# Half-head mixers, resident output weights and one query pass in a decoder-layer kernel

## Chip, cores and metric

The kernel runs on one core of a Trainium2 chip. The metric is device time of one launch, in microseconds (us). All tensors are float32; products that must be accurate are made from a high and a low part (three matmuls, `mm3`).

## What is computed

One layer of a decoder for 1,024 prompt tokens and 64 sample tokens (8 sequences of 8), cut to what matters here:

```python
proj = rmsnorm(h) @ w_in                      # retention and RWKV-7 columns
o_ret = head_norm(retention(q, k, v)) * silu(g)          # 8 heads of 64
o_rw  = (head_norm(rwkv7(r, w, k, kk, a, v)) + bonus) * g2   # 8 heads of 64
h = h + concat(o_ret, o_rw) @ w_out
xn = rmsnorm(h)                               # PEER:
s  = (xn @ wq) . keys                         # 8 heads, two halves of 128 keys
e  = 16 best of the pairs, per head           # 128 experts of 16,384 per token
h  = h + sum_e gate_e * gelu(xn . pu[e]) * pv[e]
h  = h + sigmoid(h' @ w_gate) * (p @ w_ple);  final rmsnorm
```

The RWKV-7 step is done in chunks of 128 tokens: per head a triangular system is solved level by level (blocks double in size), and a state is carried to the next chunk.

## The kernel before

The 1,088 tokens are nine tiles: 0 to 7 are the prompt (128 tokens each), 8 is the sample (64). Three stages follow one another.

**Projections (0 to about 600 us).** `group_a` makes the projections of tiles 0 and 1, 2 and 3, then 4 to 8 (lists `A0`, `A1`, `A2`). `a_ret` writes retention columns to DRAM (`rd`), `a_rw` the RWKV columns, transposed, to `fd`. Tile 0's mixer (`first_mix`) is interleaved with the second group. `c_rows` then does tile 0's output projection, residual and norm and writes the normed rows `xd`; `early` starts on that tile beside the third group.

**Mixers (`group_b`, about 600 to 1868 us).** Tiles are mixed in the order `BORDER` = 1, 8, 2, 3, ..., 7. `mixers` is `ret_mix` (load `qv`, retention, half of the output row) and then `rw_mix` (load `ft`; decay, keys and masks; the solve; state; norm; the other half). Two tiles are in flight: the one whose solve runs (`cur`) and the one that is prepared up to the solve (`nxt`). All eight heads of a tile are worked together, in tiles of 128x1024 or 128x512. A level of the solve (line 837 and on) does four heads after the other four: a transpose of Z into `Tt`, the products `pG` and `pZG`, and two VectorE steps (`G`, `Z`). The mixer's output row goes to DRAM (`od`) in two halves, and `c_rows` loads it back (`cot`) and multiplies it with `w_out`, of which it loads sixteen pieces of 256 KB (`cw`, line 609) per tile.

**The early tiles.** Tiles 0, 1 and 8 (`E0`) don't go through the dense expert pass at the end: for each of their tokens' 128 experts a row of `pu` and later one of `pv` is gathered from HBM by GpSimd (`gather`, line 1126) and used by VectorE (line 1140 for `pu`, 1154 for `pv`). Before that, `early_query` streams the query weights (sixteen times 512 KB, `ewq`, and a key block `ekT`) and makes the scores, and `topk` picks the experts. In `group_b` one step of `early` is taken per step of the mixers, at most `EB` = 150. Gathered rows have four places: two in `V`, one in `W`, one in `xy`. Tile 0's query has two weight buffers (`V`); those of tiles 1 and 8 run one after the other with one buffer (`Wq`), beside tile 0's gathers, each once its tile's rows are there (`rowed`).

**The rest (1868 us to the end).** Queries, top-k, gates and hidden products of tiles 2 to 7, the dense expert passes `ph` and `py` of tiles 4 to 7, and beside them the rest of the gathers, for tiles 2 and 3 too; then the per-layer embedding.

The order of the instructions on each engine is fixed when the program is built, by a scheduler that takes them in program order and by priorities; `early` has a later priority. On the chip each engine runs its list in order. SyncE (SP) issues most loads, in its own fixed order.

Of the kernel before, what the change touches and what calls it, by code (L numbers as in the profile page):

```python
# [17 lines left out]
D = 1024  # L18
# [167 lines left out]
IB = 2  # L186
PGT = "a"
SPL = "gv"
IE = 2
IA = 2  # L190
G2 = [4, 5, 6, 7]
RSTART = 2
RRATE = 1
# [17 lines left out]
class K:  # L211
# [28 lines left out]
    def setup(self):  # L240
# [11 lines left out]
        self.od = {t: self.dp.tile([128, D], F32, name=f"od{t}") for t in range(9)}  # L252
        self.yd = {t: self.dp.tile([128, D], F32, name=f"yd{t}") for t in range(9)}
        self.fd = self.dp.tile([128, 14, T], F32, name="fd")
# [3 lines left out]
    def setup_mix(self, es):  # L258
# [18 lines left out]
        self.Sb = [[cp.tile([128, 4, 128], F32, name=f"S{a}{b}") for b in range(2)] for a in range(3)]  # L277
# [60 lines left out]
    def group_a(self, pools, tiles, tags, then=None):  # L338
# [16 lines left out]
        yield from self.a_ret(wp, tiles, x, prepare(), tags)  # L355
        yield "rw"
        yield from self.a_rw(wp, tiles, x, tags)

    def a_ret(self, wp, tiles, x, ready, tags):
        nc, I = self.nc, self.I  # L360
        off, _ = spans(tiles)
        if True:
            for cb in range(8):
# [8 lines left out]
                if cb == 0:  # L372
                    next(ready, None)
# [30 lines left out]
    def head_norm(self, wp, p, n, eps, mk):  # L404
        nc = self.nc
        pv = p[:n].rearrange("p (h d) -> p h d", h=8)
        s = wp.tile([128, 8], F32, name="hns")
        nc.vector.tensor_reduce(s[:n], pv, axis=AX.X, op=OP.add)
        nc.vector.tensor_scalar(s[:n], s[:n], 1.0 / 64, None, op0=OP.mult)
        xc = mk("hnx").rearrange("p (h d) -> p h d", h=8)  # L410
        nc.vector.tensor_tensor(xc[:n], pv, s[:n, :, None].to_broadcast([n, 8, 64]), op=OP.subtract)
        sq = mk("hnq").rearrange("p (h d) -> p h d", h=8)
        nc.scalar.activation(sq[:n], xc[:n], AF.Square)
        ss = wp.tile([128, 8], F32, name="hnss")
        nc.vector.tensor_reduce(ss[:n], sq[:n], axis=AX.X, op=OP.add)
        r = self.rsq(wp, ss, n, 1.0 / 64, eps, 8, "hnr")
        nc.vector.tensor_tensor(xc[:n], xc[:n], r[:n, :, None].to_broadcast([n, 8, 64]), op=OP.mult)
# [18 lines left out]
    def ret_mix(self, wp, t):  # L436
# [3 lines left out]
        rt = dict(qv="Q", qkT="Z", inT="N", hnx="Tt0", hnq="Tt1") if t == 0 else dict(hnx="qkT", hnq="inT")  # L440
# [3 lines left out]
        q, k, v, gt = (qv[:n, j * 512:j * 512 + 512] for j in range(4))  # L444
        qT = mk("qkT", [128, 8, n])
        for kk in range(2):
            p = self.ps("tr").rearrange("p (a b) -> p a b", a=4)
            for j in range(4):
                nc.tensor.transpose(p[:, j, :n], qv[:n, (kk * 4 + j) * 128:(kk * 4 + j) * 128 + 128], self.c("ident")[:n, :n])
            nc.scalar.activation(qT[:, 4 * kk:4 * kk + 4, :n], p[:, :, :n], AF.Copy)  # L450
            yield
# [1091 lines left out]
```

## Time and profile before

| | us |
|---|---|
| median of three runs | 3939.46 (3925.63 to 3940.68) |
| profiled execution, its own time | 3941.76 |
| its span | 3940.0 |
| TensorE busy | 3367.7 (85%) |
| VectorE busy | 2961.7 (75%) |
| GpSimd busy | 2339.6 (59%) |
| ScalarE busy | 1225.5 (31%) |
| mean granted TensorE clock, share of full | 0.87 |
| data moved | 1107.20 MB, mean 281 GB/s |

Shares are of the whole span; the stages differ. A stretch is read from the table of windows (busy time of each engine, granted clock), what was late in it from the waits (who waited, for whom) and from the chain, which follows the work that ended last back to what released it.

### The profile page before, as it was taken

Reading aid. Unit: us, or ns where it says so; the run is one execution under the profiler, and the core shown is the slowest. Engines: PE = TensorE matmul, PEld = TensorE weight load, DVE = VectorE, ACT = ScalarE, POOL = GpSimd, SP = SyncE. Lnnn points to the kernel's source line nnn. Section 1 sums busy time; section 2 is a strip of 40 time slices with the busy share of each in tenths; the row PEclk is TensorE's granted clock in tenths of the full one; section 3 lists DMA queues with packets and bytes.
Section 4 is the critical chain, followed back from the end, with each engine's and each line's share of the span. In section 5 each row is a group of like instructions: output and inputs, shape, how many; then the busy total and the mean of one; then the engine's idle time right before and its main releaser. Section 6 shows DMA issues by size and latency. Waiting matters only on the chain.

```text
span 3940.0 us, 52682 instructions
## 1 busy us (share of the span) xinstructions
PE 3367.7 (85%) x17749; PEld 2768.7 (70%) x17749; DVE 2961.7 (75%) x5764; ACT 1225.5 (31%) x2247; POOL 2339.6 (59%) x2051
## 2 busy tenths in 40 slices
PE   8798985777869776885899899999699988999978
PEld 7687984645747664763788678888588866677757
DVE  4454488977697689886659999987777777777774
ACT  4232221011111111111232266777422333333322
POOL 5353175544454536554567757886488777777740
PEclk9799995666977567676999999999899999999989
DMA  7267568898868878789998748899899999999962
GB/s 256 72 194 234 168 209 266 277 302 267 295 229 285 299 269 283 265 278 332 331 350 295 245 171 302 306 347 344 324 343 341 334 362 357 358 362 349 339 230 70
DMA packets 473864, 1107.20 MB, mean 281 GB/s; under 512 B 74555, under 2 KB 191545, under 8 KB 467642
## 3 DMA queue, kind: packets, MB, share of 16 engines
q0 software_dynamic: 165888, 604.05, 43.0%
q1 hardware_dynamic: 245694, 393.26, 30.5%
q10 hardware_dynamic: 62012, 106.52, 7.2%
q8 instruction: 141, 2.31, 0.2%
q14 instruction: 129, 1.06, 0.1%
HBM read 997.17 MB, written 106.43 MB: 280 GB/s over the span
## 4 chain that ended last, share of the span: by engine, by line
PE 45%; DVE 22%; DMA 16%; issue 7%; POOL 6%; ACT 2%; SPq 0%; ACTq 0%; POOLq 0%; DVEq 0%
PE py L1294 14%; DVE grow L1140 4%; DVE gacc L1154 3%; PE ph L325 3%; PE ph L326 3%; PE ph L327 3%; POOL grow L1126 3%; DMA ewq<-in_wq 2%; PE epq L1194 2%; DMA grow<-in_pv,eid 2%; DMA grow<-in_pu,eid 2%; POOL vl L300 2%; DMA ft<-fd 1%; DVE oh L1240 1%; PE ewo L610 1%
## 5 line engine op out<-in xcount | busy, mean ns | idle before, releaser
L1126 POOL DMA_INDIRECT grow<-in_pv,eid x576 | 569.8, 989 | 507.3 <-DVE gacc L1154 309.4
L1126 POOL DMA_INDIRECT grow<-in_pu,eid x576 | 568.7, 987 | 435.2 <-DVE grow L1140 287.9
L1154 DVE SCALAR_TENSOR_TENSOR gacc<-grow,ac,gacc 128x1024 f32<-128x1024 f32 x571 | 731.8, 1282 | 89.5 <-DMA grow<-in_pv,eid 84.3
L1140 DVE SCALAR_TENSOR_TENSOR grow<-grow,gacc 128x1024 f32<-128x1024 f32 x576 | 691.1, 1213 | 125.0 <-DMA grow<-in_pu,eid 118.3
L1294 PE MATMUL py<-ah,vh 128*128 128x512 f32 x1024 | 408.1, 399 | 40.3 <-ACT ah L296 27.1
L1294 PE MATMUL py<-ah,vl 128*128 128x512 f32 x1024 | 407.1, 403 | 34.1 <-POOL vl L300 34.0
L325 PE MATMUL ph<-cx,uh 128*128 128x512 f32 x1024 | 406.4, 397 | 7.2 <-ACT geh L1262 7.2
L326 PE MATMUL ph<-cx,uh 128*128 128x512 f32 x1024 | 406.4, 397 | 0.0
L327 PE MATMUL ph<-cx,ul 128*128 128x512 f32 x1024 | 405.5, 396 | 1.0 <-POOL ul L300 1.0
L1294 PE MATMUL py<-al,vh 128*128 128x512 f32 x1024 | 405.3, 396 | 0.0
L300 POOL TENSOR_TENSOR vl<-vraw,vh 128x640 fp32r<-128x640 f32 (+2 forms) x224 | 325.4, 1457 | 53.1 <-ACT vh L296 49.3
L300 POOL TENSOR_TENSOR ul<-uraw,uh 128x1024 fp32r<-128x1024 f32 x128 | 308.6, 2412 | 64.5 <-ACT uh L296 62.3
L296 ACT ACTIVATE vh<-vraw 128x640 fp32r<-128x640 f32 (+2 forms) x224 | 154.9, 692 | 393.8 <-PE py L1294 238.3
L1294 PEld LDWEIGHTS py<-ah,vl 128*128 128x128 f32 x1024 | 194.1, 190 | 98.4 <-POOL vl L300 56.1
L1294 PEld LDWEIGHTS py<-ah,vh 128*128 128x128 f32 x1024 | 194.6, 190 | 96.5 <-ACT vh L296 28.7
L1298 DVE TENSOR_TENSOR yT<-yT,py 128x512 f32<-128x512 f32 x216 | 147.4, 684 | 151.5 <-PE py L1294 151.1
L325 PEld LDWEIGHTS ph<-cx,uh 128*128 128x128 f32 x1024 | 194.7, 190 | 48.4 <-ACT geh L1262 8.8
L1294 PEld LDWEIGHTS py<-al,vh 128*128 128x128 f32 x1024 | 194.0, 189 | 43.7
L327 PEld LDWEIGHTS ph<-cx,ul 128*128 128x128 f32 x1024 | 194.9, 190 | 41.6 <-POOL ul L300 1.9
L326 PEld LDWEIGHTS ph<-cx,uh 128*128 128x128 f32 x1024 | 195.0, 190 | 39.1
L296 ACT ACTIVATE uh<-uraw 128x1024 fp32r<-128x1024 f32 x128 | 135.2, 1056 | 246.1 <-PE ph L326 128.5
L300 POOL TENSOR_TENSOR wl<-wraw,wh 128x1024 fp32r<-128x1024 f32 x45 | 110.5, 2455 | 138.8 <-ACT wh L296 138.7
(400 smaller groups left out, 7833.3 us busy)
## 6 DMA issues: line engine op xcount, KB each, us to landing
uraw<-in_puT SPq DMA_DIRECT2D x128, 512.0 KB, 4.8
vraw<-in_pvd SPq DMA_DIRECT2D x152, 320.0 KB, 6.1
cw<-in_w_out SPq DMA_DIRECT2D x128, 256.0 KB, 5.1
wd<-wst ACTq DMA_DIRECT2D x32, 1024.0 KB, 13.1
wt<-wd SPq DMA_DIRECT2D x64, 512.0 KB, 8.0
wraw<-in_w_ret SPq DMA_DIRECT2D x48, 512.0 KB, 4.7
ewq<-in_wq SPq DMA_DIRECT2D x48, 512.0 KB, 6.7
gd<-geh ACTq DMA_DIRECT2D x96, 256.0 KB, 5.0
```

The lines of the kernel that those rows point to most:

```text
L296: nc.scalar.activation(hi, src, AF.Copy)
L300: nc.gpsimd.tensor_tensor(lo, src, hi.bitcast(F32), op=OP.subtract)
L325: mm(out, lh(k), rh(k), start=first and k == 0, stop=False)
L326: mm(out, lh(k), rl(k), start=False, stop=False)
L327: mm(out, ll(k), rh(k), start=False, stop=last and k == nk - 1)
L610: nc.tensor.matmul(p[:n], oT[k // 4][:, k % 4, :n], w, start=k == 0, stop=k == 7)
L1126: nc.gpsimd.indirect_dma_start(out=g, out_offset=None, in_=src, in_offset=bass.IndirectOffsetOnAxis(ap=self.eid[t][:, j:j + 1], axis=0))
L1140: nc.vector.scalar_tensor_tensor(g[:, c], g[:, c], 1.0, x[:, c], op0=OP.mult, op1=OP.mult, accum_out=hv[:, i, j:j + 1])
L1154: nc.vector.scalar_tensor_tensor(y[:, c], g[:, c], ac[:, j:j + 1], y[:, c], op0=OP.mult, op1=OP.add)
L1194: nc.tensor.matmul(p[:, :n], w[:, k], xT[:, k, :n], start=k == 0, stop=k == 7)
L1294: nc.tensor.matmul(p, lh[:, b, :], rh, start=b == 0 and j == 0, stop=b == nb - 1 and j == 2)
L1298: nc.vector.tensor_tensor(yT[:, d, :], yT[:, d, :], p, op=OP.add)
```

## The change

- A mixer's unit is now half of a tile's heads: `ret_mix` and `rw_mix` take (tile, half `g`), their tiles are half as wide, in two buffers (`BB`), and a level of the solve is one group of four heads. Two units are in flight, as two tiles were. One set of pools (`mix_pools`) serves tile 0 and `group_b`.
- The output row stays on chip (`ot`, 128x1024, two buffers): the stores to `od` and the loads `cot` are gone.
- `w_out` is loaded once in `group_b` (`wo`, eight pieces of 512 KB); only tile 0's `c_rows` still loads `cw`. All tiles but 7 end their `c_rows` in `group_b`.
- `fd` is laid out by tile, so that a tile's columns are contiguous: a load `lo` of two column blocks for both halves, `ft` of six for each half. The order of the blocks in `a_rw` (`FT`) and of the column groups in `a_ret` changes with it.
- Gathered rows have seven places in `group_b`: three of the pool `rows` (`R2`) beside the four. After the queries two more (`W2`), and for the last tile `xT`.
- Tiles 1 and 8 share one query pass: three weight buffers, each weight block used for both tiles. It begins when the rows of both are there; `group_b` takes no step of `early` until then.
- `RR` = 2 steps of `c_rows` per mixer step, from the start; `IB` 3 for 2.

In numbers of instructions: VectorE 4,542 to 4,861, GpSimd 2,056 to 2,184, ScalarE 2,609 to 2,656, TensorE 14,633 to 14,651, SP 1,098 to 972.

The core of the diff:

```diff
-IB = 2
-PGT = "a"
+IB = 3
+FT = (12, 13, 4, 5, 0, 1, 8, 9, 6, 7, 2, 3, 10, 11)
 SPL = "gv"
+BB = 2
+R2 = 3
+RR = 2
...
-RSTART = 2
-RRATE = 1
...
-        self.fd = self.dp.tile([128, 14, T], F32, name="fd")
+        self.fd = self.dp.tile([9, 128, 14, 128], F32, name="fd")
...
-    def ret_mix(self, wp, t):
+    def ret_mix(self, wp, t, g):
...
-        qv = mk("qv", [128, RET])
-        nc.sync.dma_start(qv[:n], self.rd[t][:n])
+        qv = mk("qv", [128, 4, 256])
+        nc.sync.dma_start(qv[:n], self.rd[t][:n].rearrange("p (j c) -> p j c", j=4)[:, :, g * 256:g * 256 + 256])
...
-        nc.scalar.dma_start(self.od[t][:n, :512], xf)
+        if g == 0:
+            self.ot[t] = (self.ep0.tile([128, D], F32, name="ot", tag="Wq", bufs=1) if t == 7 else
+                          self.mp.tile([128, D], F32, name="ot", bufs=2))
+        nc.vector.tensor_tensor(self.ot[t][:n, 256 * g:256 * g + 256], xf, gt, op=OP.mult)
...
-        for k in range(1 if t == 7 else 2):
-            nc.sync.dma_start(ot[k][:n], self.od[t][:n, cs[k]])
...
                 for k in range(8):
-                    w = half("cw")
-                    nc.sync.dma_start(w, I['w_out'][k, :, cs[c]])
+                    if self.wo:
+                        w = self.wo[k][:, cs[c]]
+                    else:
+                        w = half("cw")
+                        nc.sync.dma_start(w, I['w_out'][k, :, cs[c]])
                     nc.tensor.matmul(p[:n], oT[k // 4][:, k % 4, :n], w, start=k == 0, stop=k == 7)
...
+    def mix(self, tiles):
+
+        nxt = None
+        units = [(t, g) for t in tiles for g in range(2)]
+        for i, u in enumerate(units + [None]):
+            cur, nxt = nxt, self.mixers(*u) if u else None
+            live = nxt is not None
+            while live or cur is not None:
+                if cur is not None:
+                    if next(cur, "end") == "end":
+                        cur = None
+                        if units[i - 1][1]:
+                            self.mixed.append(units[i - 1][0])
+                if live:
+                    live = next(nxt, "end") != "chain"
+                yield
 
     def group_b(self, tiles, early):
...
+            for k in range(8):
+                wo.append(wp.tile([128, D], F32, name=f"wo{k}"))
+                self.nc.sync.dma_start(wo[k], self.I['w_out'][k])
+            self.wo = wo
+            for _ in self.mix(tiles):
+                for _ in range(RR):
+                    if next(rows, "end") == "end" and self.mixed and self.mixed[0] != 7:
+                        rows = self.c_rows(self.co, self.mixed.pop(0))
+                for _ in range(ERATE if self.rowed.issuperset(E0) else 0):
+                    if steps < EB:
+                        steps += 1
+                        next(early, None)
...
-        ft = wp.tile([128, 14, n], F32, name="ft")
-        nc.sync.dma_start(ft, self.fd[:, :, o:o + n])
...
+            lo = wp.tile([128, 2, n], F32, name="lo")
+            nc.sync.dma_start(lo, self.fd[t, :, 0:2, :n])
...
+        ft = wp.tile([128, 6, n], F32, name="ft", bufs=2)
+        nc.sync.dma_start(ft, self.fd[t, :, 2 + 6 * g:8 + 6 * g, :n])
...
-            for s in range(2):
-                p = self.ps("trz", hb[s]).rearrange("p (a b) -> p a b", a=4)
-                for j in range(4):
-                    nc.tensor.transpose(p[:n, j, :n], Z[:n, 4 * s + j, :n], self.c("ident", n)[:, :n])
...
+            p = self.ps("trz", "b").rearrange("p (a b) -> p a b", a=4)
+            for j in range(4):
+                nc.tensor.transpose(p[:n, j, :n], Z[:n, j], self.c("ident", n)[:, :n])
...
-    def early_query(self, wp, t, wtag, wbufs, stags):
+    def early_query(self, wp, tiles, ws, xts):
...
-            for k in range(8):
-                nc.tensor.matmul(p[:, :n], w[:, k], xT[:, k, :n], start=k == 0, stop=k == 7)
...
+            for t in tiles:
+                for k in range(8):
+                    nc.tensor.matmul(p[:, off[t]:off[t] + SIZE[t]], w[:, k], xT[t][:, k, :SIZE[t]], start=k == 0, stop=k == 7)
...
+        while not self.rowed.issuperset(E0):
+            next(g, None)
+            yield
+        w2 = (self.r2, "W2", 2)
+        for _ in self.early_query(wp, E0[1:], [(wp, "Wq", 1), w2, w2], [(wp, "xT", 1), (self.r2, "R", R2)]):
+            next(g, None)
+            yield
         for t in E0[1:]:
-            while t not in self.rowed:
+            for _ in self.early_topk(wp, t, [w2, w2]):
                 next(g, None)
                 yield
-            for _ in self.early_query(wp, t, "Wq", 1, ("Wq", "xT")):
-                next(g, None)
-                yield
+        self.rows += [w2, w2]
         yield from g
...
+            r2 = self.r2 = sb("rows", ew, side="right")
+            self.layout(r2, [("R", [128, D], F32, R2), ("W2", [128, D], F32, 2)])
+            self.rows += [(r2, "R", R2)] * R2
             late = self.group_b(BORDER, early)
```

VectorE, the mixers of tiles 1 and 8. Before, in tile 1's solve (`G`, `Z`), while tile 8 is prepared; `grow` on line 1140 is the use of a gathered `pu` row of tile 0:

```order
L851 TENSOR_TENSOR Z<-Z,pZG 128x128x2
L1140 SCALAR_TENSOR_TENSOR grow,hv<-grow,gacc 128x1024
L461 TENSOR_TENSOR inT<-pin,cstb 64x256 x2
L1140 SCALAR_TENSOR_TENSOR grow,hv<-grow,gacc 128x1024
L851 TENSOR_TENSOR Z<-Z,pZG 128x128x2
L1140 SCALAR_TENSOR_TENSOR grow,hv<-grow,gacc 128x1024
L844 TENSOR_TENSOR G_6726<-pG,cstb 128x256
L1140 SCALAR_TENSOR_TENSOR grow,hv<-grow,gacc 128x1024
L431 SCALAR_TENSOR_TENSOR qm<-qkT,cstb 128x512 x2
L1140 SCALAR_TENSOR_TENSOR grow,hv<-grow,gacc 128x1024
L844 TENSOR_TENSOR G_6768<-pG,cstb 128x256
```

The change, tile 8's second half in its solve, tile 2's first half prepared:

```order
L417 TENSOR_REDUCE hnss<-hnq 64x4
L876 TENSOR_TENSOR G<-pG,cstb 64x128
L463 TENSOR_TENSOR inT<-pin,cstb 128x256 x2
L419 TENSOR_TENSOR hnx<-hnx,hnr 64x256
L882 TENSOR_TENSOR Z<-Z,pZG 64x64x2
L410 TENSOR_REDUCE hns<-po 128x4
L511 TENSOR_TENSOR S_192<-pst,S_193 64x2x64 x2
L411 TENSOR_SCALAR hns<-hns 128x4
L512 TENSOR_TENSOR S_192<-S_192,cstb 64x2x64 x2
L876 TENSOR_TENSOR G<-pG,cstb 64x128
L413 TENSOR_TENSOR hnx<-po,hns 128x256
L1008 TENSOR_TENSOR ot<-hnx,pgt 64x256
```

The gathered rows of tile 0 are no longer between these steps: 74 of its 128 `pu` rows are used by the end of tile 1's first half, and the 75th comes after both halves of tile 8.

TensorE, the query pass (`epq`: with `ewq` the query, with `ekT` the scores). Before, tile 1's, beside tile 8's state products (`pss`, `psT`):

```order
L1194 MATMUL epq<-exT,ewq 128x128 x8
L1197 MATMUL epq<-ekT,eqT 128x128
L943 MATMUL pss<-uexp,nbk 64x512
L943 MATMUL pss<-uexp,ktk 64x512
L950 MATMUL psT<-csta,sw_7809 64x64 x8
L1194 MATMUL epq<-exT,ewq 128x128 x8
L761 MATMUL pbon<-cstb,sq 128x8 x4
L761 MATMUL pbon<-cstb,rk_7843 128x8 x4
L1197 MATMUL epq<-ekT,eqT 128x128
```

The change, tiles 1 and 8 together, beside tile 2's solve and preparation:

```order
L1234 MATMUL epq<-exT,ewq 128x128 x8
L1234 MATMUL epq<-exT,ewq 128x64 x5
L1241 MATMUL epq<-ekT,eqT 64x128
L1234 MATMUL epq<-exT,ewq 128x64 x3
L880 MATMUL pZG<-G,Tt 128x64 x4
L756 MATMUL pcs<-cstb,sg 128x129 x2
L1241 MATMUL epq<-ekT,eqT 128x128
L869 MATMUL trz<-csta,Z 128x128 x4
L874 MATMUL pG<-Z,N 128x64 x4
L1234 MATMUL epq<-exT,ewq 128x128 x8
L1234 MATMUL epq<-exT,ewq 128x64 x2
L1241 MATMUL epq<-ekT,eqT 64x128
```

Each weight block is now used for 128 and for 64 columns, one behind the other; before, tile 8's sixteen blocks came in a second pass.

SP, the beginning of `group_b`. The change:

```order
L535 DMA wraw<-in_w_rw 128x1024 x3
L1228 DMA ekT<-in_keysT 128x128 x2
L535 DMA wraw<-in_w_rw 128x1024 x11
L701 DMA wo_6582<-in_w_out 128x1024
L701 DMA wo_6584<-in_w_out 128x1024
L701 DMA wo_6586<-in_w_out 128x1024
L701 DMA wo_6588<-in_w_out 128x1024
L701 DMA wo_6590<-in_w_out 128x1024
L701 DMA wo_6592<-in_w_out 128x1024
L701 DMA wo_6594<-in_w_out 128x1024
L701 DMA wo_6596<-in_w_out 128x1024
L446 DMA qv<-rd_112 128x4x256
L732 DMA lo<-fd 128x256
L742 DMA ft<-fd 128x768 x2
L446 DMA qv<-rd_112 128x4x256
```

The eight loads of `wo` stand behind the projections' last weights (`wraw`) and ahead of tile 1's loads.

## Rows read from the trace of the kernel before

**Rows 1.** The page: busy time (share) xinstructions; chain that ended last

```profile
PE 3367.7 (85%) x17749; PEld 2768.7 (70%) x17749; DVE 2961.7 (75%) x5764; ACT 1225.5 (31%) x2247; POOL 2339.6 (59%) x2051
...
PE 45%; DVE 22%; DMA 16%; issue 7%; POOL 6%; ACT 2%; SPq 0%; ACTq 0%; POOLq 0%; DVEq 0%
```

**Rows 2.** Windows: stretch, length, busy us by engine, PEclk, DMA share, GB/s

```profile
600.00:1868.00 1268.00, 951.99 (x4988) 736.82 (x4989) 1006.97 (x1874) 176.31 (x379) 646.47 (x638) 0.68 0.83 280
600.00:930.00 330.00, 237.05 (x1199) 168.48 (x1200) 269.57 (x476) 39.66 (x87) 174.67 (x173) 0.62 0.86 277
930.00:1060.00 130.00, 101.68 (x706) 85.31 (x704) 88.65 (x109) 19.64 (x47) 55.08 (x54) 0.81 0.90 285
1290.00:1420.00 130.00, 109.54 (x485) 98.12 (x486) 79.92 (x148) 16.64 (x43) 56.29 (x59) 0.51 0.83 288
1509.00:1729.00 220.00, 187.05 (x1026) 147.90 (x1025) 190.43 (x274) 39.81 (x77) 123.92 (x119) 0.76 0.83 284
100.00:200.00 100.00, 77.38 (x529) 69.43 (x527) 47.41 (x89) 26.23 (x47) 31.48 (x28) 0.78 0.23 73
1868.00:3940.00 2072.00, 1900.23 (x8826) 1541.02 (x8824) 1641.69 (x3196) 873.30 (x1560) 1418.50 (x1154) 0.97 0.86 308
```

**Rows 3.** The chain of waits from 600 to 1870 us, by line

```profile
by line: issue 8.4%; DMA ewq<-in_wq 6.9%; DVE grow L1140 6.6%; DMA grow<-in_pv,eid 5.7%; PE epq L1194 5.3%; DVE gacc L1154 4.9%; DMA grow<-in_pu,eid 4.5%; DMA ft<-fd 4.2%; POOL grow L1126 3.6%; PE ewo L610 3.0%; DMA cw<-in_w_out 2.8%; PE pZ
```

**Rows 4.** The same chain, one piece: start us, length us, what

```profile
602.48 12.95 DMA ft<-fd
```

**Rows 5.** Windows of L1126 (gather issues) alone: GpSimd busy us (xissues)

```profile
600.00:1868.00 1268.00, 480.60 (x480) 0.68 0.83 280
```

**Rows 6.** VectorE groups, 600-1870 us: busy us, mean ns | idle before

```profile
L1154 DVE SCALAR_TENSOR_TENSOR gacc<-grow,ac,gacc 128x1024 f32<-128x1024 f32 x246 | 315.1, 1281 | 57.7 <-DMA grow<-in_pv,eid 55.9
L1140 DVE SCALAR_TENSOR_TENSOR grow<-grow,gacc 128x1024 f32<-128x1024 f32 x233 | 280.4, 1212 | 61.0 <-DMA grow<-in_pu,eid 59.4
L844 DVE TENSOR_TENSOR G<-pG,cstb 128x256 f32<-128x256 f32 x70 | 29.2, 417 | 29.4 <-PE pG L842 29.1
L851 DVE TENSOR_TENSOR Z<-Z,pZG 128x256 f32<-128x256 f32 x70 | 28.6, 413 | 11.2 <-PE pZG L849 10.6
...
L798 DVE TENSOR_TENSOR Kq<-pab,cstb 128x512 f32<-128x512 f32 x28 | 18.9, 682 | 8.2 <-PE pab L793 8.2
```

**Rows 7.** TensorE waits, same stretch: us, times, longest us

```profile
PE epq L1194 <- DMA ewq<-in_wq: 22.6, 15, 6.9
...
PE ewo L610 <- DMA cw<-in_w_out: 10.6, 10, 3.6
...
PE etr L594 <- DMA cot<-od: 7.2, 3, 3.1
```

**Rows 8.** TensorE groups, same stretch

```profile
L610 PE MATMUL ewo<-cw,coT 128*128 128x512 f32 x192 | 107.3, 667 | 8.0 <-DMA cw<-in_w_out 6.3 <-DVE S L506 0.7 <-DVE ch L613 0.7
L842 PE MATMUL pG<-Z,N 128*128 128x64 f32 x560 | 89.3, 314 | 0.0
L849 PE MATMUL pZG<-G,Tt 128*128 128x64 f32 x560 | 87.6, 313 | 3.2 <-DVE G L844 3.2
L1194 PE MATMUL epq<-exT,ewq 128*128 128x64 f32 x256 | 57.6, 412 | 18.5 <-DMA ewq<-in_wq 14.0 <-DVE Q L803 2.4 <-DVE Kq L798 2.0
L837 PE MATMUL trz<-csta,Z 128*128 128x128 f32 x280 | 55.3, 331 | 5.9 <-POOL Z L825 3.0 <-DVE Z L851 2.7
...
L1194 PE MATMUL epq<-exT,ewq 128*128 128x128 f32 x256 | 48.0, 356 | 9.3 <-DMA ewq<-in_wq 8.6 <-ACT ktk L815 0.7
```

**Rows 9.** ScalarE group, same stretch

```profile
L839 ACT ACTIVATE Tt<-trz 128x512 f32<-128x512 f32 x70 | 41.8, 598 | 232.9 <-PE trz L837 222.8 <-DVE Z L851 5.0 <-DVE hnx L513 2.7
```

**Rows 10.** DMA issues: KB each, median us to landing

```profile
ewq<-in_wq SPq DMA_DIRECT2D x48, 512.0 KB, 6.7
...
grow<-in_pv,eid POOLq DMA_INDIRECT x576, 6.6
```

**Rows 11.** VectorE timeline, first instruction of the last stage's queries

```profile
1867.72 1.22 DVE L298 TENSOR_TENSOR wql<-wqr,wqh 128x1024 fp32r<-128x1024 f32 x1
```

More of the change, by code (lines that the diff above doesn't have):

```diff
@@ L276, in setup_mix @@
         self.lnb = self.row(cp, 'ln_b')
-        self.Sb = [[cp.tile([128, 4, 128], F32, name=f"S{a}{b}") for b in range(2)] for a in range(3)]
+        self.Sb = [[cp.tile([128, 4, 128], F32, name=f"S{a}{b}") for b in range(2 - a // 2)] for a in range(3)]
         for a in self.Sb:
@@ L362, in a_ret @@
         if True:
-            for cb in range(8):
+            for i, cb in enumerate((0, 2, 4, 6, 1, 3, 5, 7)):
                 wh, wl = [], []
@@ L585, in c_rows, with load @@
         yield
-        ot = [half("cot"), self.tail if t == 7 else half("cot")]
+        o = ROWS['norm_ffn'][0]
+        def load(c):
+            g = half("cgr")
+            nc.sync.dma_start(g, I['rows'][o + 512 * c:o + 512 * c + 512].partition_broadcast(128))
+            return g
+        gr = [load(c) for c in range(2)] if self.wo else []
+        ot = self.ot.pop(t)
         oT = [wp.tile([128, 4, 128], F32, name="coT", tag="qm", bufs=2) for _ in range(2)]
-        for k in range(1 if t == 7 else 2):
-            nc.sync.dma_start(ot[k][:n], self.od[t][:n, cs[k]])
-        yield
         for k in range(2):
@@ L618, in c_rows @@
         r = self.rsq(wp, ssq, n, 1.0 / D, 1e-6, 1, "crs")
-        gr = [half("cgr") for _ in range(2)]
-        o = ROWS['norm_ffn'][0]
         for c in range(2):
-            nc.sync.dma_start(gr[c], I['rows'][o + 512 * c:o + 512 * c + 512].partition_broadcast(128))
+            if not self.wo:
+                gr.append(load(c))
             nc.vector.scalar_tensor_tensor(h[:n, cs[c]], h[:n, cs[c]], r[:n], gr[c][:n], op0=OP.mult, op1=OP.mult)
@@ L682, in group_b @@
             for _ in rows:
                 pass
-        return done + tiles[-1:]
-    def transposes_n(self, dst, src, n):
-        nc = self.nc
-        for k in range(2):
-            p = self.ps("trn").rearrange("p (a b) -> p a b", a=4)
-            for j in range(4):
-                nc.tensor.transpose(p[:n, j, :n], src[:n, 4 * k + j, :n], self.c("ident", n)[:, :n])
-            nc.scalar.activation(dst[:n, 4 * k:4 * k + 4, :n], p[:n, :, :n], AF.Copy)
-    def rw_mix(self, t):
+            for t in self.mixed[:-1]:
+                for _ in self.c_rows(self.co, t):
+                    pass
@@ new lines, in rw_mix @@
+        nc.vector.tensor_tensor(nbk[:n].rearrange("p (h d) -> p h d", h=4), pt[:n, :256].rearrange("p (h d) -> p h d", h=4),
+                                rn2[:n, :, None].to_broadcast([n, 4, 64]), op=OP.mult)
+        yield
+        N = wp.tile([128, 4, n], F32, name="N", bufs=BB)
+        p = self.ps("trn").rearrange("p (a b) -> p a b", a=4)
+        for j in range(4):
+            nc.tensor.transpose(p[:n, j, :n], Q[:n, j, 0], self.c("ident", n)[:, :n])
+        nc.scalar.activation(N[:n], p[:n, :, :n], AF.Copy)
```

613 lines of the change are left out of this document (310 added, 303 removed).

## Prediction

> **What bounds the kernel now.** The page comes first: TensorE is busy for 85% of the span, and 45% of the chain that ended last lies on it [rows 1]. That average hides two stages, so the windows come next [rows 2]. After 1868 us TensorE is busy for 1900 of 2072 us at a granted clock of 0.97: that stage is TensorE's, and the change leaves its matmuls alone. From 600 to 1868 us it is busy for 952 of 1268 at 0.68, VectorE for 1007 (79%): no engine is full, so engines wait for one another or for data. The end of this stretch is the first VectorE instruction of the last stage's queries, at 1867.7 us [rows 11]. The change is nearly all in this stretch, and its gain or loss is read there.
>
> Three readings say what is late in it. First, the chain by line [rows 3]: of 1270 us the weight loads of the early queries take 6.9% (88 us), the loads of `ft` 4.2% (53 us, the first of them 13 us long [rows 4]), those of `cw` 2.8% (36 us), gathers about 10%. Second, what the engines themselves stood still for: TensorE waited 22.6 us for `ewq`, 10.6 for `cw`, 7.2 for `cot`, 40 together [rows 7]. So most of the 177 us of loads on the chain had other work beside them, and can't all be won. Third, VectorE: of its 261 us idle, 119 stand ahead of the two gather steps [rows 6], that is 45%.
>
> Why are gathered rows late? A row's place is taken for its issue on GpSimd (480.6 us for 480, 1.0 us each [rows 5]), its landing (6.6 us [rows 10]) and VectorE's use of it (1.21 and 1.28 us [rows 6]): some 8.9 us. Four places give at most 4 / 8.9 = 0.45 rows per us. The stretch had 480 / 1268 = 0.38. The four places are nearly the limit.
>
> **The change part by part**, for the stretch from 600 us to the queries.
>
> *More and smaller instructions.* VectorE issues 319 more. A 128x256 step takes 417 ns, a 128x512 step of the same kind (PSUM in, one product) 682 [rows 6]: two halves cost 2 x 417 - 682 = 152 ns more than a whole. 319 x 0.152 = 48 us in the whole kernel, 43 of it in this stretch (eight of nine tiles are mixed there). It is certain work on an engine that is 79% busy. [...]
>
> By the order, 498 rows are used before the queries and not 503, 6 us less. VectorE's work in the stretch becomes 1007 + 43 - 6 = 1044 us.
>
> *Start.* The eight `wo` loads (4.2 MB, at the stretch's 280 GB/s [rows 2] 15 us) stand on SP ahead of tile 1's loads; part of them runs beside the last projections, and I take 8, between 0 and 15. Tile 1's first `ft` is contiguous and half as long: 7 us for 13. Together 15 us.
>
> *Tiles 1 and 8.* No step of `early` is taken until both have their rows, and the order shows no gathered row from tile 1's end to tile 8's. So four half-tile chains, one after the other, set the time, with nothing to fill VectorE. One level is a transpose (4 x 0.20 us, 55.3 / 280), its copy 0.60 [rows 9], two products of 4 x 0.16 [rows 8] and two VectorE steps of 0.42 and 0.41: 3.5 us; five levels 17. State products, state, output and norm are about ten more such hand-overs, some 20 us, and the hand-overs themselves some 6: 43 per half, an estimate. The preparation of the next half runs beside it. First preparation plus four chains: 5 x 43 = 215; then tile 8's output rows, 16 matmuls of 0.56 us (107.3 / 192 [rows 8]) with transposes and norm, about 50. I take 265 us. VectorE's own work there, counted by the order at the rows' durations, is 176: the lower bound. The upper is 330, the first window of the stretch [rows 2], which had tile 1 and most of tile 8's solve with 140 rows used between.
>
> *The query pass.* 256 + 256 matmuls, 57.6 + 48.0 = 106 us [rows 8], as before, now in one piece with three weight buffers where one made every block wait 6.7 us [rows 10]; before, it filled two windows of 130 us each at clocks of 0.81 and 0.51 [rows 2]. Bounds 106 and 260; I take 145, near the lower, since the load of a block (6.7) now lies beside the two blocks before it. VectorE does 110 us of gathers and mixing there.
>
> *The rest.* 1044 - 176 - 110 = 758 us of VectorE work. In the steady stretch from 1509 to 1729 us VectorE was busy for 190.4 of 220 [rows 2]. Seven to ten places for rows allow 0.8 rows per us and more, so the gather waits, 45% of the idle, go: 190.4 / (220 - 13) = 0.92; with TensorE's waits for `cw` and `cot` gone too I take 0.93: 815 us. Bounds: 0.866 as before, 875 us; 0.97, 781 us. Next late is then TensorE, busy for 187 of 220 us there.
>
> *The two other stages.* Tile 0's mixer in the projections has ten half levels of 3.5 us for five whole ones of 4.1 (twice the products, beside each other), beside a TensorE with 23 us free in that window [rows 2]: 0, between -15 and +14. The last stage begins with the same gather progress; it gives tile 6's 9 us of output matmuls to the stretch before, already in the 815: 0.
>
> Sum: 15 + 265 + 145 + 815 = 1240 for 1268 us, 28 less. The profiled execution took 3941.8 us, 2.3 above the median of 3939.5; against the median the forecast is 3912 us.
>
> **The rivals.** *Slower: the chains of tiles 1 and 8.* The granted clock was 0.62 in the window where they are mixed [rows 2], and sparse matmuls won't raise it; if a half takes 54 us, the two tiles take 320, and VectorE, with 424 rows left for the time after, finds TensorE slow: 0.90, 842 us. 15 + 320 + 145 + 842 = 1322, 54 more: 3993 us. For it: VectorE is idle for a third of that part even in the forecast. Against: the solve's waits before came behind gathers in VectorE's order. It decides from 293 us on for the two tiles.
>
> *Much faster.* The loads on the chain were what held it: 225 for the two tiles, 120 for the queries, 0.96 (790 us) for the rest: 1150, 118 less, 3822 us. For it: 177 us of loads on the chain. Against: only 40 us of standstill on TensorE.
>
> *No change.* VectorE bound by work: with 0.905 the rest takes 838 us, 1263 together, 3934 us. The ring of rows would then fill without being needed: the change wouldn't do what it says.
>
> **How the numbers follow.** 0.5% of the time, 20 us, is about what a measurement of this kernel can tell from no change. Forecast 0.38, much faster 0.14, no change 0.21, slower 0.27. The forecast is just beyond the bound, so a few hundredths of it count as no change: faster 0.50, same 0.23, slower 0.27. The range leaves out the ends of the two outer rivals: 3830 to 3990 us.
>
> **What would show it.** Right: VectorE's waits ahead of the gather steps fall from 119 us to under 30; TensorE no longer waits for `ewq`, `cw`, `cot`; tile 8's rows are there about 280 us after 600; one query stretch of about 145 us; VectorE above 0.9 from there to the queries, which begin near 1840 us. Wrong: gather waits remain (then landing or HBM bandwidth holds the rows), tiles 1 and 8 take over 300 us, or the last stage is longer than 2072 us.

## The result and the profile after

The changed kernel takes 3955.98 us (median of 20 runs, 3937.95 to 3993.11); the kernel before, over 20 runs, 3936.27 us (3917.51 to 3951.38). The ratio is 1.0064 with a 95% interval of 1.0042 to 1.0086: slower by some 25 us by the ratio (the medians are 20 us apart), where 28 us less were forecast. The time lies in the stated range, on the other side of no change. The profiled execution took 3947.79 us, on the lower side of its runs, with a span of 3946.0.

The page of the changed kernel, the lines that answer to [rows 1], and its two gather groups over the whole span:

```profile
PE 3404.3 (86%) x17785; PEld 2824.9 (72%) x17785; DVE 2984.6 (76%) x6083; ACT 1233.7 (31%) x2293; POOL 2346.6 (59%) x2179
...
PE 41%; DVE 22%; DMA 10%; issue 7%; POOL 6%; ACT 1%; ACTq 0%; POOLq 0%; DVEq 0%; SPq 0%
...
L1170 DVE SCALAR_TENSOR_TENSOR grow<-grow,gacc 128x1024 f32<-128x1024 f32 x576 | 684.8, 1213 | 96.1 <-DMA grow<-in_pu,eid 86.4
L1184 DVE SCALAR_TENSOR_TENSOR gacc<-grow,ac,gacc 128x1024 f32<-128x1024 f32 x571 | 732.0, 1282 | 23.1 <-DMA grow<-in_pv,eid 17.0
```

Transfers on the chain fell from 16% to 10% of the span. The first instruction of the last stage's queries, however, stands where it stood ([rows 11]: 1867.72), on VectorE's timeline:

```profile
1868.16 1.21 DVE L298 TENSOR_TENSOR wql<-wqr,wqh 128x1024 fp32r<-128x1024 f32 x1
```

So nothing was won in the stretch on which the sum was made. Its windows, cut where the first query matmul begins (934) and where the last scores are done (1070), with the last stage behind them (columns as in [rows 2]):

```profile
600.00:1868.00 1268.00, 989.98 (x5062) 784.51 (x5062) 1013.05 (x2141) 187.17 (x423) 648.96 (x745) 0.67 0.70 242
600.00:934.00 334.00, 264.58 (x1515) 187.07 (x1516) 188.40 (x421) 47.15 (x110) 85.82 (x113) 0.68 0.44 134
934.00:1070.00 136.00, 117.20 (x831) 106.91 (x830) 82.44 (x167) 23.68 (x71) 61.67 (x70) 0.89 0.82 288
1070.00:1868.00 798.00, 608.19 (x2719) 490.53 (x2718) 742.22 (x1554) 116.34 (x242) 501.47 (x563) 0.62 0.79 280
1868.00:3946.00 2078.00, 1894.19 (x8790) 1544.35 (x8790) 1642.12 (x3198) 871.09 (x1557) 1414.30 (x1153) 0.96 0.86 307
```

| stretch | forecast us | measured us |
|---|---|---|
| start, tiles 1 and 8 | 15 + 265 = 280 | 334 |
| one query pass | 145 | 136 |
| the rest, VectorE's share | 815 at 0.93 | 798 at 742 / 798 = 0.93 |
| together | 1240 | 1268 |
| last stage | 2072 | 2078 |

The query pass and the rest came in 26 us below the forecast together, the last stage 6 us above. One line, tiles 1 and 8, took 54 us more, and the gain was gone.

What went is seen in VectorE's groups in that stretch: the idle time ahead of the two gather steps fell from 119 us to 52 [rows 6], though not under the 30 that was named as a sign of being right. On TensorE no wait for `ewq`, `cw` or `cot` is left, as against [rows 7].

```profile
L1184 DVE SCALAR_TENSOR_TENSOR gacc<-grow,ac,gacc 128x1024 f32<-128x1024 f32 x241 | 308.6, 1281 | 5.8 <-DMA grow<-in_pv,eid 3.7
L1170 DVE SCALAR_TENSOR_TENSOR grow<-grow,gacc 128x1024 f32<-128x1024 f32 x224 | 266.0, 1213 | 46.3 <-DMA grow<-in_pu,eid 40.3 <-ACT gacc L1164 5.0
```

What came in its place, TensorE's three longest waits from 600 us to the queries (the first ends at 616.99 us: tile 1's `qv` stood behind the eight `wo` loads):

```profile
PE tr L451 <- DMA qv<-rd: 31.7, 1, 31.7
PE pZG L880 <- DVE G L876: 29.0, 22, 2.6
PE trz L869 <- DVE Z L882: 27.2, 19, 2.7
```

SP spent 31.6 us on issuing the eight loads. By the profile it waited 49 us ahead of and between them for the stores of the last projections (`fdst`); that can only be for room, since the weights themselves come from elsewhere.

```profile
572.19 31.62 SPq L701 DMA_DIRECT2D wo<-in_w_out  x8
SPq L701 <- DMA fd<-fdst: 48.9, 4, 27.4
```

Before, the whole-tile solve let TensorE wait 6.5 and 2.7 us at the last two places:

```profile
PE pZG L849 <- DVE G L844: 6.5, 6, 3.3
PE trz L837 <- DVE Z L851: 2.7, 3, 2.1
```

Of the 56 us that these two waits now take, 6.5 stand before 934 us, beside tiles 1 and 8, and the rest behind it, where the stretch came in below the forecast. TensorE's solve groups also became slower and idler for the same number of matmuls (compare [rows 8]: 87.6 us and 3.2 idle, 55.3 and 5.9):

```profile
L880 PE MATMUL pZG<-G,Tt 128*128 128x64 f32 x560 | 111.8, 367 | 34.8 <-DVE G L876 28.6 <-ACT hnq L415 2.8 <-DVE hns L411 2.1
L869 PE MATMUL trz<-csta,Z 128*128 128x128 f32 x280 | 67.0, 383 | 32.8 <-DVE Z L882 26.0 <-POOL Z L859 6.6
```

### The profile page after: what moved, and what is told of

Its sections match the earlier page's. It is cut to its first block, busy times and chain, and to the rows that moved or that the text cites. A ratio compares the mean times of both kernels' runs of the same rounds, so it can differ in the third digit from the quotient of the medians.

```text
span 3946.0 us, 53070 instructions
## 1 busy us (share of the span) xinstructions
PE 3404.3 (86%) x17785; PEld 2824.9 (72%) x17785; DVE 2984.6 (76%) x6083; ACT 1233.7 (31%) x2293; POOL 2346.6 (59%) x2179
## 4 chain that ended last, share of the span: by engine, by line
PE 41%; DVE 22%; DMA 10%; issue 7%; POOL 6%; ACT 1%; ACTq 0%; POOLq 0%; DVEq 0%; SPq 0%
PE py L1348 13%; DVE gacc L1184 4%; DVE grow L1170 3%; DMA grow<-in_pu,eid 3%; PE ph L325 3%; PE ph L327 3%; PE ph L326 3%; POOL grow L1156 2%; POOL vl L300 2%; PE pwt L1299 2%; DMA grow<-in_pv,eid 2%; DVE eq L1107 1%; PE ewo L633 1%; PE pq L327 1%; PE pq L325 1%
## 5 line engine op out<-in xcount | busy, mean ns | idle before, releaser
L1170 DVE SCALAR_TENSOR_TENSOR grow<-grow,gacc 128x1024 f32<-128x1024 f32 x576 | 684.8, 1213 | 96.1 <-DMA grow<-in_pu,eid 86.4
L1184 DVE SCALAR_TENSOR_TENSOR gacc<-grow,ac,gacc 128x1024 f32<-128x1024 f32 x571 | 732.0, 1282 | 23.1 <-DMA grow<-in_pv,eid 17.0
L1296 ACT ACTIVATE oh<-oh,it 128x128 f32<-128x128 f32 x512 | 161.1, 390 | 96.0 <-DVE oh L1294 84.3
```

Source lines behind the costliest of these rows:

```text
L1170: nc.vector.scalar_tensor_tensor(g[:, c], g[:, c], 1.0, x[:, c], op0=OP.mult, op1=OP.mult, accum_out=hv[:, i, j:j + 1])
L1184: nc.vector.scalar_tensor_tensor(y[:, c], g[:, c], ac[:, j:j + 1], y[:, c], op0=OP.mult, op1=OP.add)
L1296: nc.scalar.activation(oh[0][:, j], oh[0][:, j], AF.Copy, scale=it[:, s + b + j:s + b + j + 1])
```

## A second and a third profile of both kernels

> The changed kernel once more, for a second profile. The stretch to the queries of the last stage and the last stage itself come out within 10 us of 1868 and 2078 us; if the difference of the medians (20 us) lies in the last stage, it is 2085 us or more here.

> The kernel before once more, for a second profile: queries at 1860 to 1870 us, last stage 2060 to 2075 us.

> The changed kernel a third time, for a third profile: if the granted clock beside tiles 1 and 8 (0.69 and 0.63 in the two profiles, queries at 1868 and 1910 us) sets the stretch, a clock between gives a start of the queries between.

Measured: the changed kernel 4004.86 us and 3946.19 us, the kernel before 3925.48 us. The queries begin at 1910.04, 1865.49 and 1852.35 us, and the last stages take 2093, 2079 and 2071 us. The first of the three is longer than any of the 20 timed executions, so it shows how such an execution loses time, and not where the medians' 20 us lie; its expectation was off by 42 and 15 us. The queries of `r_before` came 8 us ahead of their range. The other two profiles of each kernel leave the queries at 1868 and 1865 us against 1868 and 1852, and the last stage at 2078 and 2079 against 2072 and 2071. So 6 to 8 us stand in the last stage and on average about as much before it, which two profiles each don't settle.

A good part of what the long one lost shows in 50 us in which tile 1's second half is solved and tile 8's first half prepared. Windows of the changed kernel's three profiles, in the order first, second, third (the column before the last two is the granted clock):

```profile
700.00:750.00 50.00, 48.58 (x376) 39.98 (x377) 31.92 (x86) 10.10 (x24) 9.71 (x14) 0.85 0.29 73
```

```profile
700.00:750.00 50.00, 48.44 (x244) 38.51 (x244) 21.90 (x51) 5.12 (x11) 7.49 (x11) 0.53 0.15 39
```

```profile
700.00:750.00 50.00, 48.82 (x386) 40.30 (x384) 30.59 (x84) 10.10 (x24) 9.09 (x13) 0.87 0.26 68
```

TensorE is busy for 97% of these 50 us in all three. With a clock of 0.85 and 0.87 it does 376 and 386 matmuls in them, with 0.53 it does 244. From the norm of tile 1's first half to that of its second (`pY`) go 34, 52 and 34 us: 18 of the long one's 42. Tile 8's two halves took 87 and 55 to 57 us in all three, and its last norm begins at 893.3, 918.4 and 891.9 us. The third profile's clock beside tiles 1 and 8 was 0.70, not between the first two's 0.69 and 0.63, so the expectation for a start between them was not put to the test; a high clock and an early start (0.70 and 1865 us) did go together again.

## Filling the idle time, and the loads at the start

**Rows beside tiles 1 and 8.**

```diff
-                for _ in range(ERATE if self.rowed.issuperset(E0) else 0):
-                    if steps < EB:
-                        steps += 1
-                        next(early, None)
+                ready = self.rowed.issuperset(E0)
+                if steps < EB or not ready:
+                    steps += ready
+                    next(early, None)
```

> Edit: group_b takes steps of early from its start, so tile 0's gathered rows go on beside the mixers of tiles 1 and 8; still 150 steps once both tiles have their rows. Theory 1 (the change loses in the first 345 us of the stretch what it gains behind it, since VectorE has 149 us idle there and no rows to use): about 90 rows of tile 0 fill that idle time, VectorE is over 75% busy from 600 to 945 us, tiles 1 and 8 take at most 30 us longer, and the last stage's queries begin at about 1870 us with 600 rows used instead of 498; the time is 3900 to 3940 us, as far as the last stage gains from having 100 rows less. Theory 2 (VectorE work and TensorE's clock set the stretch wherever the rows stand): the queries begin after 1930 us and the time is 3950 us or more.

Measured: 1.0091 (1.0056 to 1.0125), 3965.51 us. Queries begin at 1932.3 us with 597 rows used; the last stage, with 100 rows less to use, took 2034 us. Theory 2 had the better numbers: 64 us later, 44 us given back. The same edit with `EB = 60`:

> Edit: as e1_gathers, but only 60 steps of early once both tiles have their rows, so that by the order 512 rows are used before the last stage's queries (498 in the changed kernel). Theory 1: the same work in less idle time; queries begin at 1770 to 1810 us instead of 1868, the last stage keeps its 2078 us, the time is 3860 to 3900 us. Theory 2: queries begin at 1850 us or later, time 3940 to 3960 us.

Measured: 1.0015 (0.9990 to 1.0039), 3933.07 us: by the ratios 0.5% better than the changed kernel, no difference from the kernel before that could be told. Queries begin at 1850.5 us, 18 us earlier, where theory 1 wanted 60 to 100. Its window of tiles 1 and 8 shows why:

```profile
600.00:945.00 345.00, 242.65 (x1266) 175.35 (x1266) 281.95 (x546) 41.82 (x96) 168.52 (x194) 0.62 0.77 255
```

VectorE is as full as before the change, 282 us (281.3 in the kernel before); in the changed kernel it is not:

```profile
600.00:945.00 345.00, 275.23 (x1597) 197.40 (x1597) 196.43 (x437) 48.77 (x115) 90.67 (x119) 0.69 0.45 136
```

But the first 945 us did not hold the same mixing: tile 8's last norm began at 958 us and not at 893. From 600 us to that norm 135 rows are used, in the changed kernel 41. These 94 rows, some 117 us of VectorE, went with a delay of 65 us. The solve's steps stand behind rows in VectorE's fixed order, and TensorE's clock was 0.62 for 0.69; which of the two cost more is not shown. VectorE's idle time was not free here: the solve's chain returns to that engine again and again.

> Edit: as e7_gathers60, but beside tiles 1 and 8 only every second mixer step takes a step of early. If the rows cost the solves in proportion (65 us for some 90 rows in e7_gathers60), the time lies within 10 us of e7_gathers60 (3933 us); if only the dense rows do harm, 10 to 25 us less.

(`idle` counts the steps ahead of the gate, and every second one takes a step of `early`.) Measured: 1.0062 (1.0041 to 1.0082), 3956.5 us: worse than the full rate. Neither expectation held. Here 89 rows are used before tile 8's last norm, which began at 947 us: about half of the added rows kept most of the delay, 54 us of 65.

**The output weights.** In `e2_cw` the eight loads are left out, so `c_rows` loads `cw`; in `e3_wolate` they stand behind 30 mixer steps:

```diff
-            for _ in self.mix(tiles):
+            for i, _ in enumerate(self.mix(tiles)):
+                if i == WOAT:
+                    for k in range(8):
+                        wo.append(wp.tile([128, D], F32, name=f"wo{k}"))
+                        self.nc.sync.dma_start(wo[k], self.I['w_out'][k])
+                    self.wo = wo
```

> Edit: the output weights are not resident in group_b; every tile loads its sixteen pieces as before the change, and nothing stands ahead of tile 1's loads. Theory 1: the start gains some 15 us (TensorE's 32 us wait for tile 1's qv becomes about 15), c_rows gets back some 10 us of waits for cw: 3945 to 3965 us, as the changed kernel. Theory 3 (the eight loads at the start and their waits for the last projections are what the change lost): 3920 to 3938 us.

> Edit: the eight loads of the resident output weights are issued 30 mixer steps later, behind the first loads of tile 1. Theory 1: TensorE's 32 us wait for tile 1's qv falls to about 15, the queries begin 5 to 15 us earlier, time 3940 to 3955 us. Theory 3: 20 to 30 us, time 3925 to 3935 us.

Measured: `e2_cw` 1.0034 (1.0008 to 1.0060); its median is 3948.78 us with two executions of 4388.51 and 6870.53 us, which nothing here explains and the ratio leaves out, and 3941.91 us without them. `e3_wolate` 1.0027 (1.0005 to 1.0048), 3937.19 us. By the ratios the early loads are worth 0.37%, some 15 us, between what the two theories asked for. In `e3_wolate` tile 1's first norm began 24 us earlier, at 599.1 us, and tile 8's last 19 us earlier, but the queries only 5 us earlier than in the first profile, at 1862.9. Theory 3, by which the loads were the whole loss, is not borne out by that start. No benefit of the resident weights shows in `e2_cw`: its ratio is below the changed kernel's, and the intervals overlap.

> Edit, of the changed kernel: e7_gathers60 and e3_wolate together. If the two are independent: 1.0015 and 1.0027 against 1.0064 of the changed kernel give about 0.998 of the kernel before, some 3920 us. If the start only shifts idle time that the rows then fill: 1.0015, as e7_gathers60.

Measured: 1.0066 (1.0042 to 1.0090), 3953.62 us. The two small gains did not add up, they vanished. Its queries began at 1857.8 us and its last stage took 2098 us. Why that stage was longer is not settled.

## What the two parts that worked are worth

```diff
-            self.rows += [(r2, "R", R2)] * R2
...
-        self.rows += [w2, w2]
```

> Edit, of the changed kernel: gathered rows have the four places of the kernel before until the end; 60 steps of early, so that 512 rows are used before the queries. Theory 1 (the larger ring pays for the stretch behind tile 8): 4 places / 8.9 us = 0.45 rows per us, 440 rows need 980 us; VectorE's waits ahead of gathers return to over 100 us and the queries begin at 1930 us or later, time 4000 us or more. Rival (VectorE's work and TensorE set the stretch, more places are not needed): within 15 us of the changed kernel, 3940 to 3970 us.

Measured: 1.0359 (1.0316 to 1.0401), 4064.25 us, queries at 1943.4 us. VectorE's waits from 600 us to the queries:

```profile
DVE grow L1170 <- DMA grow<-in_pu,eid: 67.7, 72, 3.8
DVE gacc L1184 <- DMA grow<-in_pv,eid: 55.5, 65, 3.1
```

They are back at 123 us. Here, and in the next run, the scheduler put rows beside tiles 1 and 8, so the fair neighbour is `e7_gathers60` (512 rows before the queries in all three): 1.0359 against 1.0015. By that the larger ring is worth some 130 us; in the profiles 93 of them stand before the queries.

```diff
-        for _ in self.early_query(wp, E0[1:], [(wp, "Wq", 1), w2, w2], [(wp, "xT", 1), (self.r2, "R", R2)]):
-            next(g, None)
-            yield
+        for t in E0[1:]:
+            for _ in self.early_query(wp, [t], [(wp, "Wq", 1)], [(wp, "xT", 1)]):
+                next(g, None)
+                yield
```

> Edit, of the changed kernel: tiles 1 and 8 have a query pass each, with one weight buffer, as before. Theory 1 (the single pass took the weight loads off the path): the second pass adds some 100 us of one block every 8 to 10 us, queries of the last stage begin 60 to 110 us later, time 4000 to 4060 us. Rival (the passes hide behind mixing and gathers): 3945 to 3975 us.

Measured: 1.0400 (1.0368 to 1.0432), 4089.25 us, queries at 2039.4 us; TensorE waited for `ewq` again:

```profile
PE epq L1234 <- DMA ewq<-in_wq: 32.1, 18, 3.0
```

Against `e7_gathers60` that is about 150 us, but the edit takes away two things at once, the shared pass and two of the three weight buffers. The waits for `ewq` are 32 us of the 189 by which the queries are later than there; where the others come from is not shown. Both parts do help, by more than the prediction gave them. They need not add up, and no run takes both back. Since the kernel before lacks both and is as fast as `e7_gathers60`, the rest of the change should cost about as much as they bring together.

> Edit, of the changed kernel: tile 1's query pass begins when tile 1's rows are there, tile 8's when its own are, each with the three weight buffers; tile 0's rows go on from the start of group_b; 80 steps, 512 rows before the queries. Theory 5 (the wait for both tiles, with VectorE and the query weights idle, is the loss): queries of the last stage at 1800 us or before, time 3880 to 3910 us. Rival (TensorE at its granted clock is nearly full beside tiles 1 and 8, so a query put there delays them, and the second pass costs its 106 us of weight blocks again): 3950 us or more.

(Tile 1's pass starts as soon as tile 1 has its rows, the gate tests `E0[1]`, and the buffers stay three.) Measured: 1.0162 (1.0115 to 1.0210), 3996.09 us, queries at 1911.9 us. The rival's time came. The edit begins tile 1's pass earlier and splits the pass, so which of the two costs the 58 us over `e7_gathers60` is not separated; together they are worse than waiting for both tiles.

## What the halves cost

The other side was tried in the kernel before: the levels of the solve for four heads, then for the other four.

```diff
-        for li, m in enumerate(LEVELS):
+        for s in range(2):
+            for li, m in enumerate(LEVELS):
...
-            for s in range(2):
-                p = self.ps("trz", hb[s]).rearrange("p (a b) -> p a b", a=4)
+                p = self.ps("trz", hb[s]).rearrange("p (a b) -> p a b", a=4)
```

> Edit, of the kernel before: the levels of the solve are done for the first four heads and then for the other four, one chain behind the other as in the change; everything else is the kernel before (whole-tile instructions, one query buffer, four row places). Theory 4 (halves in line expose each level's hand-overs: in the changed kernel TensorE stands 56 us more ahead of trz and pZG than before): the stretch from 600 us to the queries grows by 30 to 60 us, TensorE's idle ahead of trz and pZG rises from 13 us to over 50, time 30 to 60 us above the kernel before. Rival: the gathers and the next tile's preparation fill the gaps, less than 10 us.

Measured: 1.0203 (1.0164 to 1.0243), 4005.25 us, 76 us above its kernel before. TensorE's waits in the solve, from 600 to 1870 us:

```profile
PE pZG L847 <- DVE G L843: 32.0, 23, 4.7
PE trz L836 <- DVE Z L849: 24.2, 17, 4.5
```

Before they were 6.5 and 2.7 us; in the changed kernel 29.0 and 27.2. So this alone, with whole-tile instructions everywhere else, makes as long waits there as the change has, and costs 2% in the kernel before. The profiled execution reached the queries 82 us later, with 38 rows more, which took 48 us of VectorE and which the last stage gave back in part.

Two attempts to take the line out of the changed kernel failed:

```diff
-            cur, nxt = nxt, self.mixers(*u) if u else None
+            cur, nxt = nxt, [self.mixers(t, g) for g in range(2)] if t is not None else []
...
-                if live:
-                    live = next(nxt, "end") != "chain"
+                cur = [m for m in cur if next(m, "end") != "end"]
+                if live and next(live[0], "end") == "chain":
+                    live.pop(0)
```

> Edit, of the changed kernel: the two halves of a tile are in their solve together, level by level in turn as before the change, with four half-tile buffers; to make room the output weights are not resident (as e2_cw) and gathered rows have five places and not seven until the queries are done. 512 rows before the queries. Theory 4 (halves in line cost the change its gain): TensorE's idle ahead of trz and pZG falls from 69 us to under 30, tiles 1 and 8 are done 40 us earlier or more, time 40 to 80 us under e2_cw (3949 us): 3870 to 3910 us. Rival (what bounds is TensorE's clock and VectorE's work, not the line of hand-overs): 3930 to 3960 us.

> Edit: e11_pair, and group_b takes steps of early from its start as e7_gathers60 (60 steps behind the gate, 512 rows). Theory 4: the gap-filling rows cost the paired solve less than they cost halves in line (65 us there), so another 10 to 30 us under e11_pair. Rival: rows in VectorE's order delay the solve by as much as they fill, as in e7_gathers60: within 15 us of e11_pair.

Measured: 1.0388 (1.0353 to 1.0424), 4079.59 us, and 1.0406 (1.0373 to 1.0439), 4088.24 us. Both times are far off every expectation. The waits did fall in `e11_pair`, from 56 us (78 in `e2_cw`) to 25, under the 30 of theory 4:

```profile
PE trz L864 <- DVE Z L877: 13.1, 9, 3.5
PE pZG L875 <- DVE G L871: 11.4, 6, 4.0
```

But tile 8's last norm began at 927 us (910 in `e2_cw`), and in `e12_pair_gathers` at 986. The paired halves share one PSUM place behind the solve, one `ft` buffer and several small tiles, and gathered rows lose two places. The runs change too much to tell the theories apart: the waits were shorter here and the kernel slower.

> Edit, of e2_cw (the changed kernel without resident output weights): three half-tile units in flight and not two, in the room of those weights: the part behind the solve of one half (state, output, norm) runs beside the solve of the next half and the preparation of a third. 404 rows are used before the queries by the order, 487 in e2_cw. Theory 4 (halves in line cost the change its gain): tiles 1 and 8 are done 30 us earlier or more (tile 8's last norm at 880 us or before, 910 in e2_cw), the queries begin 60 us earlier or more, time 3890 to 3930 us if the last stage takes the 80 rows without cost, up to 3960 if it pays for them. Rival (TensorE at its low clock bounds those tiles whatever the order): tile 8's last norm within 15 us of 910 us, time 3945 us or more.

> Edit: e13_stagger with two steps of early per mixer step and not one (453 rows before the queries). If e13_stagger only moved rows into the last stage, this gives the same time; if the rows fit into the idle time of the shorter stretch, 10 to 20 us less.

Here the solve ends with a mark of its own (`yield "tail"`), and the tail of one half, the solve of the next and the preparation of a third advance together. Measured: 1.0238 (1.0202 to 1.0274), 4028.46 us, and 1.0190 (1.0150 to 1.0230), 4005.68 us. Tile 8's last norm began at 918 and 907 us against 910 in `e2_cw`: for tiles 1 and 8 the rival held, overlapping the halves does not shorten them. The window of `e13_stagger` fits that TensorE bounds them, busy for 290 of 345 us at 0.67 of its clock:

```profile
600.00:945.00 345.00, 290.08 (x1598) 206.45 (x1599) 199.25 (x453) 48.93 (x117) 93.29 (x120) 0.67 0.44 135
```

Its queries did begin 84 us earlier than in `e2_cw`, at 1798.7 us, but with 83 rows fewer, and the last stage took 2229 us for 2077. A row moved into that stage cost 1.8 us there, more than the 1.25 us that VectorE needs for it. In its profile TensorE waits longer in the last stage for GpSimd's weight splits (18.4 us in `e2_cw`):

```profile
PE ph L327 <- POOL ul L300: 62.9, 23, 7.0
```

## Why the prediction was wrong

**What bounds the kernel.** Right that the stretch before the queries decides, and that gathers and query weights were late in it: undoing the larger ring or the query pass costs 130 or 150 us against `e7_gathers60`.

**More and smaller instructions.** 48 us were forecast for VectorE. Without the two gather groups it was busy for 2984.6 - 684.8 - 732.0 = 1567.8 us, against 2961.7 - 691.1 - 731.8 = 1538.8 by the page before: 29 us. That was not the loss.

```profile
L1154 DVE SCALAR_TENSOR_TENSOR gacc<-grow,ac,gacc 128x1024 f32<-128x1024 f32 x571 | 731.8, 1282 | 89.5 <-DMA grow<-in_pv,eid 84.3
L1140 DVE SCALAR_TENSOR_TENSOR grow<-grow,gacc 128x1024 f32<-128x1024 f32 x576 | 691.1, 1213 | 125.0 <-DMA grow<-in_pu,eid 118.3
```

**Start.** 15 forecast, 17 measured to TensorE's first work on tile 1 (616.99 us). That was luck: 8 of the 15 were for the eight loads as a transfer, but with the loads later (`e3_wolate`) tile 1's first norm begins 24 us earlier. The wait for their room was not in the sum.

**Tiles 1 and 8** is the step that failed: "First preparation plus four chains: 5 x 43 = 215", with which the two tiles came to 265 us; they took 317. The sum prices tile 8's halves like those of a prompt tile. The stretch, cut where TensorE starts on tile 1, at the four `pY` norms (717.5, 751.3, 838.3 and 893.3 us) and where the query pass begins:

```profile
617.00:717.50 100.50, 74.10 (x360) 63.17 (x361) 78.26 (x169) 14.51 (x34) 49.99 (x59) 0.55 0.69 221
717.50:751.30 33.80, 33.02 (x259) 26.39 (x258) 22.81 (x65) 7.28 (x18) 7.83 (x12) 0.90 0.30 71
751.30:838.35 87.05, 74.48 (x416) 44.16 (x415) 42.11 (x93) 9.10 (x23) 8.45 (x14) 0.71 0.31 78
838.35:893.25 54.90, 50.58 (x333) 32.86 (x332) 32.09 (x67) 9.50 (x22) 9.98 (x15) 0.69 0.22 58
893.25:934.00 40.75, 32.39 (x153) 20.48 (x154) 9.84 (x23) 6.76 (x14) 6.17 (x9) 0.87 0.33 97
```

| | forecast us | measured us |
|---|---|---|
| preparation and tile 1's first half | 86 | 100 |
| tile 1's second half | 43 | 34 |
| tile 8's two halves | 86 | 142 |
| to the query pass | 50 | 41 |

Tile 8's halves alone are 56 us over, and TensorE is busy for 125 of their 142 us, VectorE for 74. The kernel solves only two levels for tile 8 (`if smp and m >= 8: break`), not five, but each of its eight sequences has a state of its own. Four groups of matmuls, which only this tile has, take 82 us of TensorE here (tiles `sr`, `psr`, `pss`, `psT`, a line each; behind the length stand TensorE's busy time and its matmuls):

```profile
600.00:934.00 334.00, 35.53 (x384) 0.68 0.44 134
600.00:934.00 334.00, 10.87 (x16) 0.68 0.44 134
600.00:934.00 334.00, 26.84 (x32) 0.68 0.44 134
600.00:934.00 334.00, 8.41 (x64) 0.68 0.44 134
```

In the trace of the kernel before, which the prediction had, they take 80 us, spread over a longer stretch and with query and gathers beside them:

```profile
600.00:1100.00 500.00, 32.52 (x384) 0.68 0.87 283
600.00:1100.00 500.00, 14.54 (x16) 0.68 0.87 283
600.00:1100.00 500.00, 25.23 (x32) 0.68 0.87 283
600.00:1100.00 500.00, 8.14 (x64) 0.68 0.87 283
```

In the sum they were part of "about ten more such hand-overs, some 20 us" per half. Tile 1's output rows, 16 us of matmuls from 751 to 772 us, stood between tile 8's levels too and were in no term. The lower bound was taken from VectorE's work, 176 us; TensorE's, 265 us of the 334, was not counted. Little of the excess is waits between the levels of halves in line: TensorE's are 6.5 us there. The level has a misreading too: a product is eight matmuls in [rows 8] (560 for the 70 copies of [rows 9]), not four, so that by the same rows a level is 4.8 us and five are 24, not 17. Tile 1's second half stayed under its 43 all the same.

**The query pass** and **the rest** held: 136 us for 145, and 798 us at 0.93 for 815 at 0.93. The rest was shorter because VectorE had 742 us to do there and not 758.

**The last stage** was forecast to stay: 2072 us, against 2078 and 2079 in the first and third profile. One new wait was missed: in the 500 us from 1868 TensorE waited for GpSimd's splits of the up weights

```profile
PE ph L327 <- POOL ul L300: 14.2, 10, 5.7
```

where the kernel before waited 1.0 us:

```profile
PE ph L327 <- POOL ul L300: 1.0, 2, 0.6
```

**The rivals.** The slower one named the right stretch, tiles 1 and 8, and its 320 us are close to the 317 measured. In that there is luck, since it had every half at 54 us, because the clock would stay at 0.62. That was a guess: from 600 to 945 us it was 0.69, tile 1's second half took 34 us at 0.90, and tile 8's halves took 87 and 55 at 0.71 and 0.69. Its price of 54 us for the whole was too high by about half, since it also let the rest fall to 0.90, which stayed at 0.93. The bound of 330 us for the two tiles stood in the text.

**Open.** How the cost divides, in the changed kernel itself, between tile 8's work on TensorE with nothing else to fill the time, levels in line, the loads at the start and the added instructions: no run took tile 8's work out of that place. `e8_serial` shows the levels in line in the kernel before, the paired runs did not separate them. No version run here beats both kernels; `e7_gathers60` equals the kernel before within its interval.

## What to carry to other kernels

Price a chain that is taken out of company by the busy time of every engine that it uses, unit by unit, and not by a sum of hand-overs for one unit times their number: one of the two tiles here was of another kind. Two groups that took turns in a solve hid each other's waits: in the kernel before, running them one behind the other raised TensorE's waits there from 9 to 56 us and cost 2%. And rows that fill an engine's idle time can delay the chain that made it idle: 94 rows, some 117 us of fillers, went with 65 us more for the chain, and half as many still with 54.

## What was not expected of the hardware

The same program, at the same place (700 to 750 us) with TensorE equally busy, 97%, was granted clocks of 0.85, 0.53 and 0.87 in three executions, and did 376, 244 and 386 matmuls. Why is not known. The kernel before had 0.62 there at 83% busy:

```profile
700.00:750.00 50.00, 41.59 (x212) 28.85 (x210) 47.45 (x89) 4.21 (x7) 25.92 (x27) 0.62 0.88 277
```

The changed kernel's 20 runs span 55 us, those of the kernel before 34. That the clock in such a stretch makes the difference is a guess that no run tests.
